# Gate and up projections of a feed-forward layer in pairs by Strassen's algorithm, weight sums by adding transfers and VectorE

## The chip, the cores and the metric

One core of a Trainium2 chip runs the whole program. The metric is the device time of one launch in microseconds (us). TensorE (PE) multiplies, VectorE (DVE) and ScalarE (ACT) work on the results, GpSimd (POOL) does a few products, and SyncE (SP) issues the loads.

## What is computed

A decoder trunk of two layers on 512 tokens of 1024 features, all in float32. Each layer mixes the tokens in four head groups, adds the result to the residual, and then runs the feed-forward part that the change touches:

```python
y = rmsnorm(x, norm2)                          # (512, 1024)
x = x + (silu(y @ w_gate) * (y @ w_up)) @ w_down   # w_gate, w_up: (1024, 2816)
```

## The kernel before

Activations are held feature-major: the residual is eight tiles xT[k] of 128 features x 512 tokens. A weight matrix comes in units of 128 x 1024 floats, 512 KB each: for gate or up, one unit holds 128 output columns, as 8 chunks (k) of 128 x 128. To keep float32 accuracy each operand is split into a high part, rounded to the fast format fp32r, and a low part, the rest; a product is the sum of three matmuls for each k (high·high, low·high, high·low), so a unit has 24 matmuls of 128 x 128 weights against 512 tokens (function `prod`, lines 321, 323 and 325).

Weights are run by the class `Weights`. `load` (L288) issues on SP into one of two raw tiles "wr"; `split` makes the high part by ACT (`S.copy`, L299) and the low part by DVE (L300) into one of three pairs of tiles "wh", "wl"; `get` first prepares until three units stand ready. A load waits until the DVE split has read its raw tile.

The feed-forward part runs over three groups of hidden units, `HID_PARTS` = 0 to 7, 8 to 14, 15 to 21. For each unit j it multiplies gate (g) and up (u), scales the gate's sum by the norm's factors r (DVE, L1145), takes Silu (ACT, L1146), multiplies by r on POOL (L1147), multiplies up's sum by that (DVE, L1150), and splits the product in high and low (ACT L1152, DVE L1153). Then eight units of w_down (d) multiply the group's units, and DVE adds the sums to xT (L1164). The first gate and up unit of a layer wait for nothing but the unscaled operand (`first_two`), and r comes later.

Instructions are written in program order, and a scheduler that has its own idea of durations sets each engine's order when the program is built. That order is fixed in the program: an engine runs its list from the top, and an instruction whose input isn't there holds up all that stand behind it.

## Time and profile before

| | |
|---|---|
| median of 3 runs | 1247.04 us (1246.91 to 1247.53) |
| the profiled execution | 1247.17 us |
| its span, first to last instruction | 1245.5 us |
| granted TensorE clock, mean | 0.998 |
| PE busy | 1231.8 us, 99% |
| DVE, ACT, POOL busy | 698.4, 539.4, 164.6 us |
| weight units loaded | 110 MB moved in all, 88 GB/s |

The first lines of the page give each engine's busy time; the chain of work that ended last says through which engines the end can be followed back. A matmul's row lasts longer than the distance to the next one, since matmuls overlap: what one costs is the distance between two starts in the timeline.

### The profile page before, as it was taken

The numbers are of one execution on the slowest core, as the hardware profiler recorded it, in microseconds if no ns is written. First come the engines' busy times: TensorE is split into PE (matmuls) and PEld (weight loads), VectorE is DVE, ScalarE is ACT, GpSimd is POOL, SyncE is SP. The second block draws the span as 40 slices with busy tenths as digits, with TensorE's granted clock in tenths as the row PEclk, the third lists the DMA queues.
The fourth block names the chain that finished last, engine by engine and source line by source line (L and its number), as shares of the span: only waits on it lengthen the run. The fifth ranks groups of instructions, "written<-read, shape, count | busy, mean of one in ns | idle before, by whom it ended". The sixth has DMA issues, their size and how long they took to land.

```text
span 1245.5 us, 16270 instructions
## 1 busy us (share of the span) xinstructions
PE 1231.8 (99%) x6412; PEld 1009.6 (81%) x6412; DVE 698.4 (56%) x1162; ACT 539.4 (43%) x896; POOL 164.6 (13%) x151
## 2 busy tenths in 40 slices
PE   9999999999999999999999999999999999999997
PEld 7887787788888888888888978777888888888886
DVE  7877798584333334334557678966643343434344
ACT  6557866563222222223444587574532122213232
POOL 0103210001100110111301132000111011101111
PEclk9999999999999999999999999999999999999999
DMA  6222221123323333332333221122233333233321
GB/s 206 93 85 69 60 69 52 52 85 101 102 89 98 102 93 93 102 102 89 98 89 98 86 69 43 53 67 68 86 101 102 91 96 102 89 100 99 97 89 68
DMA packets 32908, 110.00 MB, mean 88 GB/s; under 512 B 4096, under 2 KB 4256, under 8 KB 32832
## 3 DMA queue, kind: packets, MB, share of 16 engines
q1 hardware_dynamic: 31824, 108.28, 28.1%
q8 instruction: 50, 0.82, 0.3%
q10 hardware_dynamic: 432, 0.60, 0.2%
q14 instruction: 26, 0.21, 0.1%
q0 software_dynamic: 576, 0.08, 0.0%
HBM read 106.79 MB, written 2.10 MB: 87 GB/s over the span
## 4 chain that ended last, share of the span: by engine, by line
PE 84%; DVE 7%; ACT 4%; issue 2%; POOL 1%; DMA 0%; SPq 0%; DVEq 0%; POOLq 0%
PE g L325 6%; PE g L323 6%; PE u L323 6%; PE u L325 6%; PE g L321 6%; PE u L321 6%; PE d L325 5%; PE d L323 5%; PE d L321 5%; PE ft L323 3%; PE ft L321 3%; PE ft L325 3%; PE sm L729 2%; PE oa L321 1%; PE oa L325 1%
## 5 line engine op out<-in xcount | busy, mean ns | idle before, releaser
L299 ACT CAST wh<-wr 128x1024 fp32r<-128x1024 f32 (+2 forms) x206 | 210.2, 1022 | 540.4 <-issue 342.5
L300 DVE TENSOR_TENSOR wl<-wr,wh 128x1024 fp32r<-128x1024 f32 (+2 forms) x206 | 244.7, 1188 | 58.2 <-ACT wh L299 57.9
L321 PE MATMUL d<-uh,wh 128*128 128x512 f32 x296 | 115.1, 389 | 0.0
L323 PE MATMUL d<-uh,wl 128*128 128x512 f32 x296 | 115.1, 389 | 0.0
L325 PE MATMUL d<-ul,wh 128*128 128x512 f32 x296 | 115.1, 389 | 0.0
L1150 DVE TENSOR_TENSOR ft<-u,fs 128x512 f32<-128x512 f32 x44 | 30.4, 692 | 131.6 <-PE u L325 127.4
L1164 DVE TENSOR_TENSOR xT<-xT,d 128x512 f32<-128x512 f32 x40 | 27.5, 687 | 104.6 <-PE d L325 104.6
L1147 POOL TENSOR_TENSOR fs<-fs,n_1r 128x512 f32<-128x512 f32 x22 | 38.3, 1743 | 331.9 <-ACT fs L1146 331.9
L1147 POOL TENSOR_TENSOR fs<-fs,n_0r 128x512 f32<-128x512 f32 x22 | 38.3, 1743 | 331.7 <-ACT fs L1146 331.7
L325 PE MATMUL g<-n_0l,wh 128*128 128x512 f32 x176 | 68.5, 389 | 0.0
L323 PE MATMUL g<-n_0h,wl 128*128 128x512 f32 x176 | 68.5, 389 | 0.0
L321 PE MATMUL g<-n_0h,wh 128*128 128x512 f32 x176 | 68.5, 389 | 0.0
L325 PE MATMUL u<-n_0l,wh 128*128 128x512 f32 x176 | 68.5, 389 | 0.0
L321 PE MATMUL u<-n_0h,wh 128*128 128x512 f32 x176 | 68.5, 389 | 0.0
L323 PE MATMUL u<-n_0h,wl 128*128 128x512 f32 x176 | 68.5, 389 | 0.0
L321 PE MATMUL g<-n_1h,wh 128*128 128x512 f32 x176 | 68.5, 389 | 0.0
L323 PE MATMUL g<-n_1h,wl 128*128 128x512 f32 x176 | 68.5, 389 | 0.0
L325 PE MATMUL g<-n_1l,wh 128*128 128x512 f32 x176 | 68.5, 389 | 0.0
L321 PE MATMUL u<-n_1h,wh 128*128 128x512 f32 x176 | 68.5, 389 | 0.0
L323 PE MATMUL u<-n_1h,wl 128*128 128x512 f32 x176 | 68.5, 389 | 0.0
L325 PE MATMUL u<-n_1l,wh 128*128 128x512 f32 x176 | 68.5, 389 | 0.0
L323 PEld LDWEIGHTS d<-uh,wl 128*128 128x128 f32 x296 | 55.6, 188 | 11.6
(669 smaller groups left out, 2815.6 us busy)
## 6 DMA issues: line engine op xcount, KB each, us to landing
wr<-in_weights_dram SPq DMA_DIRECT2D x168, 512.0 KB, 3.5
wr<-in_weights_dram SPq DMA_DIRECT2D x32, 448.0 KB, 3.2
xT<-in_x_dram SPq DMA_DIRECT2D x8, 256.0 KB, 5.6
out_dram<-foo SPq DMA_DIRECT2D x7, 256.0 KB, 2.4
wr<-in_weights_dram SPq DMA_DIRECT2D x6, 256.0 KB, 4.3
posi<-in_positions_dram ACTq DMA_DIRECT2D x1, 256.0 KB, 3.1
out_dram<-foo ACTq DMA_DIRECT2D x1, 256.0 KB, 2.8
fkb<-jrr POOLq DMA_DIRECT2D x8, 4.0 KB, 2.5
```

The source lines that it names most:

```text
L299: S.copy(h[:, c], raw[:, c])
L300: V.tensor_tensor(lo[:, c], raw[:, c], h.bitcast(F32)[:, c], op=ALU.subtract)
L321: PE.matmul(ps, lhsT=wh[:, k, c0:c0 + P], rhs=ah, start=k == 0, stop=False)
L323: PE.matmul(ps, lhsT=wl[:, k, c0:c0 + P], rhs=ah, start=False, stop=False)
L325: last = PE.matmul(ps, lhsT=wh[:, k, c0:c0 + P], rhs=al, start=False, stop=k == n - 1)
L729: PE.matmul(ps[:, :n], lhsT=q[:d, blk(qb)], rhs=k[:d, :n], start=i == 0, stop=i == len(terms[h]) - 1)
L1147: G.tensor_tensor(s, s, r, op=ALU.mult)
L1150: V.tensor_tensor(t, pu, s, op=ALU.mult)
L1164: V.tensor_tensor(xT[m], xT[m], ps, op=ALU.add)
```

## The change

Of the 22 gate and up units of each layer, units 0 to 3 stay as they are ("plain"). The other 18 go in nine pairs, for gate and for up: a pair's weights, 1024 input features x 256 columns, are cut into four quadrants (two feature halves x two column units), and the normalised activations into four (two feature halves x two token halves of 256). Seven products of a quadrant sum against an activation sum (Strassen's algorithm in Winograd's form), each 4 chunks x 3 matmuls of 256 tokens, give what eight would; `pair_products` accumulates them in two PSUM tiles and adds the partial results by three ACT copies and three DVE additions.

The sums of activations are made once a layer (`Halves`), one of four chunk pairs behind each plain unit, on ACT and DVE, from activations that are already multiplied by r, so POOL's product is gone for the pairs.

The sums of weights are made as they arrive. For each product of a pair (gate, then up) SP loads the tiles x and z (and for gate a third, v, which serves both); then POOL issues two transfers of 128 x 512 floats (256 KB) that add another quadrant from memory onto half of x and half of z; two DVE additions make y from x and z. The four parts X, Y, Z and V (two quadrants each, V one) are split in high and low as before. X, Y and Z go round the three pairs of tiles that plain units use, V has its own. The raw tiles x, z, v and y go round six tiles of the ring that held the normalised operand before (`pair_raw`); by this round, x of an up product lands in the tile that held z of the up product before.

The hidden groups become 0 to 7, 8 to 15, 16 to 21: two, four and three pairs.

```diff
@@ -51,7 +51,11 @@
 FRONT_COLS = (GR, GR + 128, SZ, SZ + 128) + tuple(SXBC + 128 * j for j in range(6))
 RINGS = dict(a=8, b=8, c=8, l=8, rg=2, m=2, gv=2, fv=2, as_=4, at=4, g=6, f=6)
 ACT_SET = "natural_log_exp_and_others"
-HID_PARTS = ((0, 8), (8, 15), (15, 22))
+HID_PARTS = ((0, 8), (8, 16), (16, 22))
+
+PLAIN = 4
+HALF = KC // 2
+PAIR_AHEAD = 3
 
 
 def _rope_inv():
@@ -100,12 +104,22 @@
             for i in range(2):
                 add(wout[r0:r0 + 256, 512 * i:512 * i + 512])
         for j0, j1 in HID_PARTS:
-            for j in range(j0, j1):
+            for j in range(j0, min(j1, PLAIN)):
                 add(I["w_gate"][l][:, j * P:j * P + P])
                 add(I["w_up"][l][:, j * P:j * P + P])
+
+            paired[len(units)] = (j1 - max(j0, PLAIN)) // 2, not j0
+            for j in range(max(j0, PLAIN), j1, 2):
+
+                quad = lambda n, r, c: I[n][l][r * D // 2:(r + 1) * D // 2, (j + c) * P:(j + c + 1) * P]
+                for n in ("w_gate", "w_up"):
+                    add(quad(n, 0, 0), quad(n, 0, 1))
+                    add(quad(n, 0, 1), quad(n, 1, 0))
+                    if n == "w_gate":
+                        add(quad("w_gate", 1, 1), quad("w_up", 1, 1))
             for m in range(KC):
                 add(I["w_down"][l, j0 * P:j1 * P, m * P:m * P + P])
-    return np.stack(units), shapes
+    return np.stack(units), (shapes, paired)
 
 
 def _columns(I):
@@ -163,6 +177,15 @@
 
         def ps_acc(name):
             return pa.tile([P, T], F32, tag="pa", name=name)
+
+        slot = [0]
+
+        def act_tile(name, dt=F32R, i=None):
+
+            if i is None:
+                i = slot[0]
+                slot[0] = (i + 1) % 8
+            return ap.tile([P, 1024], dt, tag=f"ap{i}", name=name)
 
         def tmp(tag, name, cols=T, dt=F32, parts=P):
...
             def prefetch(self, n):
-                while (self.n < len(shapes) or self.loaded) and len(self.ready) < n:
+                while (self.n < len(shapes) or self.loaded or self.plan) and len(self.ready) < n:
+                    if not self.loaded and self.n in paired:
+                        self.plan = self.pairs(*paired.pop(self.n))
+                    if self.plan and not self.loaded:
+                        if next(self.plan, None) is None:
+                            self.plan = None
+                        continue
                     for _ in self.split():
                         pass
 
             def get(self):
-                self.prefetch(AHEAD + 1)
+                self.prefetch((PAIR_AHEAD if self.plan else AHEAD) + 1)
                 return self.ready.pop(0)
+
+
+            def pair_raw(self, name):
+                self.raws += 1
+                if self.raws <= 2:
+                    return wp.tile([P, 1024], F32, tag="wr", bufs=RAWS, name=name)
+                return act_tile(name, F32, (self.raws - 3) % 6)
+
+            def pair_part(self, src, name):
+
+                n, i = src.shape[1], self.parts % 4
+                self.parts += 1
+                h, lo = (act_tile(f"{name}{c}", F32R, 6 + j) if i == 3 else
+                         wp.tile([P, 1024], F32R, tag=f"w{c}", bufs=PARTS, name=f"{name}{c}")
+                         for j, c in enumerate("hl"))
+                S.copy(h[:, :n], src)
+                V.tensor_tensor(lo[:, :n], src, h.bitcast(F32)[:, :n], op=ALU.subtract)
+                self.ready.append(tuple(t[:, :n].rearrange("p (k c) -> p k c", c=P) for t in (h, lo)))
+
+            def pair_load(self, both):
+
+                i, wt = self.n, I["weights"]
+                tail = wt[i + 2][:, 0:512] if both else wt[i - 1][:, 512:1024]
+                x, z = self.pair_raw(f"px{i}"), self.pair_raw(f"pz{i}")
+                nc.sync.dma_start(x, wt[i])
+                nc.sync.dma_start(z, wt[i + 1])
+                nc.gpsimd.dma_start(x[:, 512:1024], tail, accum_op=ALU.add)
+                nc.gpsimd.dma_start(z[:, 0:512], wt[i][:, 0:512], accum_op=ALU.add)
+                v = None
+                if both:
+                    v = self.pair_raw(f"pv{i}")
+                    nc.sync.dma_start(v, wt[i + 2])
+                self.n += 3 if both else 2
+                return i, x, z, v
+
+            def pairs(self, n, first):
+
+                if first:
+                    self.raws = 0
+                loads, v = [self.pair_load(True)], None
+                for p in range(2 * n):
+                    i, x, z, vn = loads.pop(0)
+                    v = v if vn is None else vn
+                    self.pair_part(x, f"pX{i}")
+                    yield True
+                    y = self.pair_raw(f"py{i}")
+                    V.tensor_tensor(y[:, 0:512], x[:, 512:1024], x[:, 0:512], op=ALU.add)
+                    V.tensor_tensor(y[:, 512:1024], y[:, 0:512], z[:, 512:1024], op=ALU.add)
+                    self.pair_part(y, f"pY{i}")
+                    yield True
+                    self.pair_part(z, f"pZ{i}")
+                    if p + 1 < 2 * n:
+                        loads.append(self.pair_load(p % 2 == 1))
+                    yield True
+                    self.pair_part(v[:, blk(p % 2, 512)], f"pV{i}")
+                    yield True
...
+        def prod_half(ps, w, act, first=True):
+
+            wh, wl = w
+            for k, (ah, al) in enumerate(act):
+                PE.matmul(ps, lhsT=wh[:, k, :], rhs=ah, start=first and not k, stop=False, skip_group_check=True)
+                PE.matmul(ps, lhsT=wl[:, k, :], rhs=ah, start=False, stop=False, skip_group_check=True)
+                PE.matmul(ps, lhsT=wh[:, k, :], rhs=al, start=False, stop=k == HALF - 1, skip_group_check=True)
+
+        class Halves:
+
+
+
+            def __init__(self, l, g0, r):
+                self.l, self.g0, self.r = l, g0, r
+                names = ("11", "22", "21", "d1", "d2", "d3", "d4")
+                self.act = {n: [] for n in names}
+                self.homes = [t for t in ("c", "l") for _ in range(8)] + ["at"] * 4 + ["as_"] * 4 + ["gv"] * 2 + ["fv"] * 2
+                self.count = 0
+
+            def part(self, name):
+                self.count += 1
+                return [tmp(self.homes.pop(), f"b{name}{c}{self.l}_{self.count}", dt=F32R) for c in "hl"]
+
+            def split(self, src, dst):
+                h, lo = dst
+                S.copy(h, src)
+                V.tensor_tensor(lo, src, h.bitcast(F32), op=ALU.subtract)
+
+            def chunk(self, k):
+                xn = []
+                for i, tag in ((k, "a"), (k + HALF, "b")):
+                    t = tmp(tag, f"xn{self.l}_{i}")
+                    V.scalar_tensor_tensor(t, xT[i], col(self.g0 + i), self.r, op0=ALU.mult, op1=ALU.mult)
+                    xn.append(t)
+                lo, hi = slice(0, 256), slice(256, 512)
+                (b11, b12), (b21, b22) = ((t[:, lo], t[:, hi]) for t in xn)
+                n, d = tmp("g", f"bn{self.l}_{k}"), tmp("g", f"bd{self.l}_{k}")
+                V.tensor_tensor(n[:, lo], b11, b12, op=ALU.subtract)
+                V.scalar_tensor_tensor(n[:, hi], n[:, lo], -1.0, b22, op0=ALU.mult, op1=ALU.subtract)
+                V.tensor_tensor(d[:, lo], b22, b12, op=ALU.subtract)
+                V.scalar_tensor_tensor(d[:, hi], n[:, hi], -1.0, b21, op0=ALU.mult, op1=ALU.subtract)
+                if k % 2 == 0:
+                    self.b11 = self.part("s")
+                at = slice(256 * (k % 2), 256 * (k % 2) + 256)
+                self.split(b11, [t[:, at] for t in self.b11])
+                self.act["11"].append([t[:, at] for t in self.b11])
+                for src, (m, o) in ((n, ("d1", "d2")), (xn[1], ("21", "22")), (d, ("d3", "d4"))):
+                    dst = self.part(m)
+                    self.split(src, dst)
+                    self.act[m].append([t[:, lo] for t in dst])
+                    self.act[o].append([t[:, hi] for t in dst])
+
+        def pair_products(nm, b):
+
+
+            lo, hi = slice(0, 256), slice(256, 512)
+            pa_, pb_ = ps_mix(f"{nm}a"), ps_mix(f"{nm}b")
+            t1, t2 = tmp("f", f"{nm}1"), tmp("f", f"{nm}2")
+            halves = lambda w: [[t[:, 4 * i:4 * i + 4, :] for t in w] for i in range(2)]
+            a11, s1 = halves(W.get())
+            prod_half(pa_[:, lo], a11, b["11"])
+            S.copy(t1[:, lo], pa_[:, lo])
+            prod_half(pb_[:, lo], s1, b["d1"])
+            S.copy(t2[:, hi], pb_[:, lo])
+            s2, s4 = halves(W.get())
+            prod_half(pa_[:, lo], s2, b["d2"], False)
+            S.copy(t1[:, hi], pa_[:, lo])
+            prod_half(pb_[:, lo], s4, b["22"], False)
+            V.tensor_tensor(t1[:, hi], t1[:, hi], pb_[:, lo], op=ALU.add)
+            s3, a12 = halves(W.get())
+            prod_half(pa_[:, lo], s3, b["d3"], False)
+            V.tensor_tensor(t2[:, hi], t2[:, hi], pa_[:, lo], op=ALU.add)
+            prod_half(pb_[:, hi], a12, b["21"])
+            V.tensor_tensor(t1[:, lo], t1[:, lo], pb_[:, hi], op=ALU.add)
+            prod_half(pa_[:, lo], W.get(), b["d4"], False)
+            return t1, t2, pa_[:, lo]
@@ -1135,7 +1297,7 @@
             r = None
             for j0, j1 in HID_PARTS:
                 us = []
-                for j in range(j0, j1):
+                for j in range(j0, min(j1, PLAIN)):
                     pg, pu = ps_proj(f"g{l}_{j}"), ps_mix(f"u{l}_{j}")
                     if r is None:
                         r = norm2.first_two(pg, pu, KC - 2, with_col=False)
@@ -1152,6 +1314,24 @@
                     S.copy(uh, t)
                     V.tensor_tensor(ul, t, uh.bitcast(F32), op=ALU.subtract)
                     us.append((uh, ul))
+                    if j == 0:
+                        quads = Halves(l, 16 + l * 8, r)
+                    quads.chunk(j)
+                lo, hi = slice(0, 256), slice(256, 512)
+                for j in range(max(j0, PLAIN), j1, 2):
+                    s1, s2, end = pair_products(f"g{l}_{j}", quads.act)
+                    S.activation(s1, s1, AF.Silu)
+                    S.activation(s2[:, hi], s2[:, hi], AF.Silu, scale=-1.0)
+                    silu = S.activation(s2[:, lo], end, AF.Silu, scale=-1.0)
+                    t1, t2, end = pair_products(f"u{l}_{j}", quads.act)
+                    V.tensor_tensor(t1, t1, s1, op=ALU.mult)
+                    V.scalar_tensor_tensor(t2[:, hi], t2[:, hi], -1.0, s2[:, hi], op0=ALU.mult, op1=ALU.mult)
+                    V.scalar_tensor_tensor(t2[:, lo], end, -1.0, s2[:, lo], op0=ALU.mult, op1=ALU.mult)
+                    for i, t in enumerate((t1, t2)):
+                        uh, ul = tmp("a", f"uh{l}_{j + i}", dt=F32R), tmp("b", f"ul{l}_{j + i}", dt=F32R)
+                        S.copy(uh, t)
+                        V.tensor_tensor(ul, t, uh.bitcast(F32), op=ALU.subtract)
+                        us.append((uh, ul))
                 if j1 == HC:
                     with tc.issue_after(silu.ins):
```

Where the order of the engines changes, two places matter. In the rows, the numbers behind a name are layer, unit and a buffer's number; px, pz, pv, py are the raw tiles, pXh and pXl the split parts.

**DVE, at the last plain unit, before the first pair.** Before (unit 3 of layer 0, and on to unit 4):

```order
L1153 TENSOR_TENSOR ul0_2_3059<-ft0_2_3022,uh0_2_3058 128x512
L1145 TENSOR_TENSOR ft0_3_3094<-g0_3_3062,n2_0r_2899 128x512
L300 TENSOR_TENSOR wl43_3102<-wr43_3099,wh43_3101 128x1024
L1150 TENSOR_TENSOR ft0_3_3094<-u0_3_3063,fs0_3_3095 128x512
L300 TENSOR_TENSOR wl44_3139<-wr44_3136,wh44_3138 128x1024
L1153 TENSOR_TENSOR ul0_3_3131<-ft0_3_3094,uh0_3_3130 128x512
L1145 TENSOR_TENSOR ft0_4_3166<-g0_4_3134,n2_0r_2899 128x512
L300 TENSOR_TENSOR wl45_3174<-wr45_3171,wh45_3173 128x1024
```

and in the changed kernel, from the same unit on (line numbers are those of the changed kernel):

```order
L387 TENSOR_TENSOR py42_3157<-px42_3116 128x512
L1312 TENSOR_TENSOR ft0_3_3152<-u0_3_3115,fs0_3_3153 128x512
L388 TENSOR_TENSOR py42_3157<-py42_3157,pz42_3117 128x512
L445 SCALAR_TENSOR_TENSOR xn0_3_3203<-xT3_86,pcv_91,n2_0r_2875 128x512
L1315 TENSOR_TENSOR ul0_3_3200<-ft0_3_3152,uh0_3_3199 128x512
L357 TENSOR_TENSOR pY42l_3161<-py42_3157,pY42h_3160 128x1024
L357 TENSOR_TENSOR pZ42l_3165<-pz42_3117,pZ42h_3164 128x1024
L445 SCALAR_TENSOR_TENSOR xn0_7_3205<-xT7_90,pcv_91,n2_0r_2875 128x512
L450 TENSOR_TENSOR bn0_3_3207<-xn0_3_3203 128x256
L452 TENSOR_TENSOR bd0_3_3208<-xn0_7_3205,xn0_3_3203 128x256
L451 SCALAR_TENSOR_TENSOR bn0_3_3207<-bn0_3_3207,xn0_7_3205 128x256
L439 TENSOR_TENSOR bsl0_8_3099<-xn0_3_3203,bsh0_8_3098 128x256
```

The fourth chunk of the activation sums (xn0_3, xn0_7 and what follows) stands behind ft0_3, which waits for the last plain matmul; the first pair product needs bsl0_8, the last row here.

**DVE, in an up product of a pair.** Before (unit 10 of layer 0):

```order
L1153 TENSOR_TENSOR ul0_9_3819<-ft0_9_3782,uh0_9_3818 128x512
L1145 TENSOR_TENSOR ft0_10_3854<-g0_10_3822,n2_0r_2899 128x512
L300 TENSOR_TENSOR wl65_3862<-wr65_3859,wh65_3861 128x1024
L1150 TENSOR_TENSOR ft0_10_3854<-u0_10_3823,fs0_10_3855 128x512
L300 TENSOR_TENSOR wl66_3899<-wr66_3896,wh66_3898 128x1024
L1153 TENSOR_TENSOR ul0_10_3891<-ft0_10_3854,uh0_10_3890 128x512
L1145 TENSOR_TENSOR ft0_11_3926<-g0_11_3894,n2_0r_2899 128x512
```

and in the changed kernel, from the end of the gate product of units 12 and 13 into their up product (73 is that up product's own weights; px75 and px78 are the raw tiles of the next pair's gate and up, and px78 lies where pz73 lay):

```order
L357 TENSOR_TENSOR pZ73l_4597<-pz73_4471,pZ73h_4596 128x1024
L357 TENSOR_TENSOR pV73l_4628<-pv70_4352,pV73h_4627 128x512
L357 TENSOR_TENSOR pX75l_4658<-px75_4600,pX75h_4657 128x1024
L481 TENSOR_TENSOR u0_121_4625<-u0_121_4625,u0_12b_4624 128x256
L388 TENSOR_TENSOR py75_4687<-py75_4687,pz75_4601 128x512
L387 TENSOR_TENSOR py78_4817<-px78_4724 128x512
L484 TENSOR_TENSOR u0_122_4626<-u0_122_4626,u0_12a_4623 128x256
L357 TENSOR_TENSOR pY75l_4691<-py75_4687,pY75h_4690 128x1024
L486 TENSOR_TENSOR u0_121_4625<-u0_121_4625,u0_12b_4624 128x256
L1328 SCALAR_TENSOR_TENSOR u0_122_4626<-u0_122_4626,g0_122_4502 128x256
```

The first addition of py78, which needs px78 with its added half, stands ahead of the addition at L484, which the up product's own PSUM tile waits for.

## Rows read from the trace of the kernel before

**Rows 1.** The page: busy time, share of the span, instructions; and the chain by engine.
```profile
PE 1231.8 (99%) x6412; PEld 1009.6 (81%) x6412; DVE 698.4 (56%) x1162; ACT 539.4 (43%) x896; POOL 164.6 (13%) x151
...
PE 84%; DVE 7%; ACT 4%; issue 2%; POOL 1%; DMA 0%; SPq 0%; DVEq 0%; POOLq 0%
```

**Rows 2.** Busy time by engine over one gate and up unit (us).
```profile
core 0: us, PE busy (x) PEld busy (x) DVE busy (x) ACT busy (x) POOL busy (x), PEclk, DMA share, GB/s
425.70:436.60 10.90, 10.90 (x50) 9.03 (x49) 4.46 (x6) 3.16 (x4) 1.80 (x1) 1.00 0.32 98
```

**Rows 3.** Waits of SP's queue: us in total, times, longest us.
```profile
SPq L288 <- DVE wl L300: 998.2, 186, 14.4
```

**Rows 4.** Timeline of PE, unit u and the next g: start us, us, engine, line.
```profile
429.70 0.39 PE L321 MATMUL u<-n_0h,wh 128*128 128x512 f32 x1
...
434.24 0.39 PE L325 MATMUL u<-n_0l,wh 128*128 128x512 f32 x1
434.46 0.39 PE L321 MATMUL g<-n_0h,wh 128*128 128x512 f32 x1
```

**Rows 5.** Timeline of PE, matmuls against 256 columns.
```profile
85.30 0.28 PE L334 MATMUL fvp<-wh,n_0l 128*128 128x256 f32 x1
85.42 0.28 PE L332 MATMUL fvp<-wh,n_0h 128*128 128x256 f32 x1
...
88.90 0.28 PE L334 MATMUL fvp<-wh,n_0l 128*128 128x256 f32 x1
```

**Rows 6.** Timeline of DVE, two in a row: the second starts 1.15 after the first.
```profile
446.67 1.22 DVE L300 TENSOR_TENSOR wl<-wr,wh 128x1024 fp32r<-128x1024 f32 x1 [0.37 <-ACT wh L299]
447.82 0.69 DVE L1153 TENSOR_TENSOR ul<-ft,uh 128x512 fp32r<-128x512 f32 x1
```

**Rows 7.** Groups by shape: count, busy us, mean ns; then idle before.
```profile
L386 DVE SCALAR_TENSOR_TENSOR n_0l<-xT,pcv,n_0h 128x512 fp32r<-128x512 f32 x16 | 11.7, 748 | 0.8 <-ACT n_0h L385 0.6
L811 DVE TENSOR_TENSOR xT<-xT,dl 128x256 f32<-128x256 f32 x4 | 1.7, 421 | 3.8 <-PE dl L325 3.8
...
L299 ACT CAST wh<-wr 128x1024 fp32r<-128x1024 f32 x168 | 176.2, 1051 | 425.5 <-issue 259.2 <-PE d L325 83.7 <-PE g L325 27.7
L1152 ACT CAST uh<-ft 128x512 fp32r<-128x512 f32 x44 | 27.2, 617 | 4.0 <-DVE ft L1150 4.0
L1015 ACT ACTIVATE fv<-fvp,n_0c 128x256 f32<-128x256 f32 x4 | 1.9, 475 | 4.0 <-PE fvp L334 3.9
```

**Rows 8.** Timeline of PE, the first gate matmul of layer 0.
```profile
259.53 0.39 PE L321 MATMUL g<-n_0h,wh 128*128 128x512 f32 x1
```

**Rows 9.** Timeline of DVE at the first units of layer 0; in brackets the wait.
```profile
277.99 1.23 DVE L300 TENSOR_TENSOR wl<-wr,wh 128x1024 fp32r<-128x1024 f32 x1 [0.23 <-ACT wh L299]
281.30 0.69 DVE L1150 TENSOR_TENSOR ft<-u,fs 128x512 f32<-128x512 f32 x1 [2.08 <-POOL fs L1147]
```

**Rows 10.** Timeline: a last matmul, and the DVE instruction that waited for it.
```profile
1226.48 0.28 PE L325 MATMUL dl<-ul,wh 128*128 128x256 f32 x1
...
1226.80 0.42 DVE L811 TENSOR_TENSOR xT<-xT,dl 128x256 f32<-128x256 f32 x1 [1.61 <-PE dl L325]
```

**Rows 11.** DMA issues: line's tensors, queue, count, KB each, median us to landing.
```profile
wr<-in_weights_dram SPq DMA_DIRECT2D x168, 512.0 KB, 3.5
wr<-in_weights_dram SPq DMA_DIRECT2D x32, 448.0 KB, 3.2
xT<-in_x_dram SPq DMA_DIRECT2D x8, 256.0 KB, 5.6
out_dram<-foo SPq DMA_DIRECT2D x7, 256.0 KB, 2.4
```

**Rows 12.** Timeline of POOL: a DMA issue behind what it waited for.
```profile
47.77 0.54 POOL L1039 DMA_DIRECT2D fkb<-jrr  x1 [0.29 <-POOL fkb L1038]
```

**Rows 13.** DMA issues from POOL between 123 and 128 us.
```profile
w<-in_gla_gate_w_dram POOLq DMA_DIRECT2D x1, 8.0 KB, 2.3
```

More of the change, by code (lines that the diff above doesn't have):

```diff
@@ L67, in _weights @@
 def _weights(I, depth=2):
-    units, shapes = [], []
+    units, shapes, paired = [], [], {}
     def add(*ws):
@@ L133, in _pieces, with trunk @@
     return out
-def trunk(tc, I, out, shapes, depth=2):
+def trunk(tc, I, out, shapes, paired, depth=2):
     nc = tc.nc
@@ L147, in trunk @@
         xp = pool("resid")
-        ap = pool("act", bufs=8)
+        ap = pool("act")
         wp = pool("weights", bufs=3)
@@ L279, in __init__ @@
             def __init__(self):
-                self.loaded, self.ready, self.n = [], [], 0
+                self.loaded, self.ready, self.n, self.plan, self.raws, self.parts = [], [], 0, None, 0, 0
             def load(self, parts=1):
@@ L382, in chunk @@
                 src = xT[k] if src is None else src
-                ah = ap.tile([P, T], F32R, tag="ah", name=f"{name}h{k}")
-                al = ap.tile([P, T], F32R, tag="al", name=f"{name}l{k}")
+                both = act_tile(f"{name}h{k}")
+                ah, al = both[:, 0:T], both[:, T:2 * T]
                 high = S.activation(ah, src, AF.Copy, scale=g)
@@ L446, in mix_operand @@
         def mix_operand(src, name):
-            h = ap.tile([P, T], F32R, tag="ah", name=f"{name}mh")
-            lo = ap.tile([P, T], F32R, tag="al", name=f"{name}ml")
+            both = act_tile(f"{name}mh")
+            h, lo = both[:, 0:T], both[:, T:2 * T]
             S.copy(h, src)
@@ L827, in last_part @@
             for m in range(KC):
-                xg.append(ap.tile([P, T], F32, tag="ah", name=f"xg{m}"))
+                xg.append(act_tile(f"xg{m}", F32)[:, 0:T])
                 ps, w = ps_proj(f"dl_{m}"), W.get()
@@ L1189 @@
     with tile.TileContext(nc) as tc:
-        trunk(tc, I, out, shapes)
+        trunk(tc, I, out, *shapes)
     r = run_bass_kernel_spmd(nc, [arrays], core_ids=[0])
```

## The prediction

> **What bounds the kernel now.** I read the page's busy times and chain first: TensorE is busy for 99% of the span, and 84% of the chain that ended last lies on it [rows 1]. So the time is a count of matmuls times their distance, and a change helps if it makes fewer columns and PE still never waits. The windows then show what room the others have: over one gate and up unit DVE is busy 4.46 us of 10.90 and ACT 3.16 [rows 2]. The waits of SP show that loads stand ready early: its queue waits 998 us for DVE to free a raw tile [rows 3]. What the transfers take is hidden today.
>
> **Fewer columns on PE.** From the first to the last of these rows are 21 starts in 434.46 − 429.70 = 4.76 us, 0.2267 us for a matmul against 512 tokens [rows 4]. Against 256, the 30 starts between 85.30 and 88.90 give 0.120 [rows 5]: a little over half. Two plain units are 48 matmuls, 48 × 0.2267 = 10.88 us. A pair product is 7 products × 4 chunks × 3 = 84 matmuls, 84 × 0.120 = 10.08 us. There are 9 pairs × gate and up × 2 layers = 36, so the gain is 36 × 0.80 = **28.8 us**. The down matmuls only move between groups (8, 8, 6): nothing on a full PE. The Trainium skill (TensorE: Matmul & The Clock Gate, Back-to-back issue gap) gives a lone gap of N/2.4 + 2.5 ns, which I work out as an estimate of 215.8 and 109.2 ns; by it the gain would be 42.8 us. The rows don't bear that out, and I go by 28.8.
>
> **What DVE and ACT get.** Rows that follow one another start 0.07 us before the one ahead has ended: 1024 wide every 1.15 us [rows 6], so 512 wide 0.62 (0.69 less 0.07), with a column factor 0.68 and 256 wide 0.36 [rows 6, 7]. A pair's two products give DVE six 1024-wide splits (6.9), two 512-wide (1.2), four additions for y (2.5), six on PSUM (2.2), and three multiplications and two splits for the result (2.6): 15.4 us of 20.16. ACT has six 1.05, two 0.62, six copies of some 0.45, Silu and two casts: 13. Both fit; what counts is where they stand in order. POOL's product falls away, which was on no path.
>
> **A wait before the first pair.** The first unit's matmuls begin at 259.53 [rows 8], so the plain units end at 259.53 + 4 × 10.88 = 303.05. DVE writes the first up product at 281.30 [rows 9]. From there its list up to the first part of y holds 18 instructions of 0.62, 6 of 0.68, 15 of 0.36 and 3 of 1.15: 24.1 us, to 305.4, 2.4 after PE has ended the plain units. Only then come ft0_3 and ten more rows, 7.0 us together, to bsl0_8, the last chunk of the first product's operand: 312.4. PE has 18 matmuls that need only the first three chunks (2.2 us), then waits. The other 66 take 7.9, and the copies between them, which a late product no longer hides (ACT's cast of the next weights stands among them), some 1.5 more: 321.8 instead of 313.1, less 0.6 for five matmuls that the order takes from the next product. That is 8.1 a layer, **+16.2 us**. The least is 5.7 a layer, if DVE isn't behind at 303.05 (8.1 less 2.4), the most 9.6, if the copies cost twice as much.
>
> **A loop through the raw tiles.** Time 0 is the first matmul of an up product; a group of 12 takes 1.44, so the fifth ends at 7.20 and the seventh, which accumulates onto what L484 reads, should begin at 8.64. DVE's list has the first y addition for the next up product just ahead of L484. That addition needs the next x, and x lands in the tile of this product's z. In the gate product before, at its 7.20 + 0.2 for the signal (1226.48 + 0.12 to 1226.80 [rows 10]), DVE still has a 1024-wide split to end; L484 is over at about 8.6, ACT's Silu at 9.0, its cast of z at 10.05, DVE's split of z at 11.3: 1.2 in the up product's time. SP's load takes 3.5 [rows 11], with 0.05 for the signal to 4.75. POOL wakes 0.29 later [rows 12] and issues the adding transfer, which takes A. At 5.04 + A the addition (0.62) and L484 (0.42) can go. They had to begin by 7.55, so **PE waits A − 2.5** in that product. Behind L484 DVE holds the split of Y, due 4 us later, and behind POOL's transfer the one for z, due later still; these have cover. The loop closes over z's split again, so it costs this in every pair but the last of a group: 5 a layer (units 8, 10, 12, 16, 18), 10 in all. In the first of units 4 to 7 the addition stands behind L484: nothing is counted there.
>
> A is not in this trace. Nearest below is a store of 256 KB, 2.4 us [rows 11]; nearest in kind a load by POOL of 8 KB, 2.3 us [rows 13]. 448 and 512 KB by SP differ by 0.3 [rows 11], so 256 KB are worth 1.2 and a plain load by POOL 2.3 + 1.2 = 3.5. An addition must read its target too: if that costs the transfer again, 4.7. Loads of 256 KB in the opening crowd took 5.6 [rows 11], the upper end. I take **A = 3.7**, near the row's 3.5, since only the second read is missing there. Then PE waits 1.2 in 10 products: **+12 us**. The Trainium skill (DMA: Bandwidth & Descriptors, Anatomy of one DMA) fits 2.0 us + bytes/436e3 for transfers from GpSimd; as an estimate 2.6 us here, with which this term would be 1 us; no run here shows an adding transfer.
>
> In a group's first pair the gate's y addition stands ahead of z's split too: its x waits for Z's split 2.5 after the down part, so it comes at 2.5 + 0.05 + 3.5 + 0.29 + 3.7 = 10.0 in the gate product, and the z split ends at 10.0 + 0.62 + 0.4 + 1.15 = 12.2, or 2.1 instead of 1.2: 0.9 × 2 groups × 2 layers = **+3.6**.
>
> **Sum.** −28.8 + 16.2 + 12 + 3.6 = +3.0. The profiled execution took 1247.17 us (span 1245.5), 0.13 above the median of the runs. The forecast is **1250.2 us**.
>
> **Rivals.**
> - *The transfers keep up.* A of 2.4 to 2.8: the loop costs 0 to 3, and −28.8 + 16.2 leaves −12.6: **1235** to 1238. For it: a store of this size takes 2.4. Against: POOL's own transfers need 2.3 for 8 KB.
> - *The first pair isn't held.* If ACT and DVE reach the fourth chunk in time, and the start costs at most 4 in all where I count 16.2, 1250.2 − 12.2 = **1238**. Against: the list is fixed, and DVE is full from 281.
> - *The adding transfers are slow* (the other side in full). The seventh group of each up product waits for POOL's transfer. The loop passes the gain where 10 (A − 2.5) + 4 × (A − 2.8) reaches 12.6, at A = 3.5. At A = 4.5 it costs 20 + 6.8: **1261**; at 5.6, 31 + 11.2: **1277**. For it: two loads of 512 KB and another addition are under way at the same time, where today one is.
> - *DVE falls behind.* With 15.4 of 20.2 us in strict order, every signal adds; 0.3 us more in each of 18 pairs on top of my forecast gives **1256**, and a granted clock at the lower of its two levels (1.2 instead of 2.4 GHz) after the wait in front of the first pair would add to it. The rows show the clock at 1.00 [rows 2], never after a wait of 7 us.
>
> **How the numbers follow.** My forecast, A from 3.0 to 4.5, has 0.42: 1240 to 1261, of which I give 0.02 to faster, 0.12 to no change, 0.28 to slower. Transfers that keep up: 0.26, faster. The start not held: 0.09, of which 0.08 faster and 0.01 unchanged. Slow transfers: 0.16, slower. DVE behind: 0.07, of which 0.01 unchanged. A measurement here tells 0.2%, 2.5 us, from no change. So faster 0.36, same 0.14, slower 0.50. The range is **1234 to 1264**: from A = 2.4 to 4.7. It leaves out most of the slow transfers, and what lies below 1234 if both the first two rivals hold, under 2 in 10 together.
>
> **What would show it.** In the changed profile: pair matmuls 0.120 apart; a stretch of some 7 us in each layer, after the fourth plain unit, in which PE does nothing and waits for DVE's low parts of the activation sums (their names begin with bs and bd); POOL's 256 KB transfers with a time to landing of 3 to 4.5; and PE's waits in the up products of units 8, 10, 12, 16 and 18, right before the seventh group, with DVE's y addition ended just before. I am wrong if PE waits elsewhere (on ACT's copies, or on weights at the start of a product), or if these transfers land within 2.5 us.

## The result, and the profile after

The changed kernel takes **1321.69 us** (median of 4 runs, 1318.49 to 1322.87) beside 1247.28 for the kernel before on the same chip: a ratio of 1.0592, 95% interval 1.0573 to 1.0612. It is 74 us slower, where 3 were forecast. The profiled execution took 1322.36 us, its span is 1320.6.

The page of the changed kernel: busy time, share of the span, instructions; PE's granted clock in 40 slices; the chain by engine and by line.

```profile
PE 1240.7 (94%) x7702; PEld 1077.1 (82%) x7702; DVE 863.0 (65%) x1476; ACT 650.0 (49%) x1126; POOL 166.4 (13%) x187
...
PEclk9999999998999899989999999999989989899999
...
PE 53%; issue 15%; DMA 12%; DVE 11%; ACT 6%; POOL 2%; SPq 0%; DVEq 0%; POOLq 0%; ACTq 0%
```

Against [rows 1] PE fell from 99% of the span to 94%, and from 84% of the chain to 53%. DMA, 0% of the chain before, has 12. And the clock has slices below 9: PE's 1240.7 us busy hold fewer columns than the 1231.8 of before, partly at the lower clock.

Busy time by stretch in the changed kernel (PE, PEld, DVE, ACT, POOL, then granted clock, DMA share, GB/s): the start of the first pair, and most of the four pairs of the middle group.

```profile
304.00:320.00 16.00, 8.09 (x42) 7.25 (x41) 13.74 (x24) 8.07 (x15) 4.88 (x4) 0.71 0.89 249
410.00:500.00 90.00, 80.69 (x614) 79.33 (x614) 54.88 (x79) 41.96 (x71) 12.15 (x14) 0.92 0.57 141
```

Two places lose time: a stop of some 8 us at the first pair, with DVE busy for 13.74 of 16 us, and a steady loss over all pairs, in which no engine is full (PE 80.69 and DVE 54.88 of 90). PE's waits name them. Columns: us in total, times, longest.

```profile
PE g_4a L417 <- ACT bsh L438: 11.7, 2, 6.2
PE u_8a L417 <- DVE u L484: 7.5, 2, 3.8
...
PE u_12a L417 <- DVE u L484: 6.0, 2, 3.8
PE g_4a L419 <- DVE bsl L439: 4.7, 2, 2.4
```

The first and the last are the fourth chunk of the activation sums. The others stand before the seventh product of an up product, behind L484, where the prediction had put them; but they are 1.7 to 3.8 us instead of 1.2, and there are 15 of them instead of 10. From PE's timeline I added up how long each of the 36 pair products takes beyond its 84 × 0.120 = 10.08 us: **100.8 us** in all. Of these, 64.9 are waits (16.4 of them for the activation sums of the first pairs), 26.9 are matmuls at 0.21 instead of 0.12, the rest small steps. Less the 28.8 of gain that makes 72.0 of the 74.4 found.

What L484 stands behind is seen on DVE in one up product (start, us, what, in brackets the wait):

```profile
478.73 0.69 DVE L388 TENSOR_TENSOR py<-py,pz 128x512 f32<-128x512 f32 x1 [2.17 <-DMA pz<-in_weights_dram]
479.99 0.69 DVE L387 TENSOR_TENSOR py<-px 128x512 f32<-128x512 f32 x1 [0.56 <-DMA px<-in_weights_dram]
480.60 0.41 DVE L484 TENSOR_TENSOR u<-u,u_12a 128x256 f32<-128x256 f32 x1
```

The first is the second y addition of the next gate product, waiting for z; the second is the addition that the prediction looked at, waiting for x. Over the ten up products that the prediction counted, DVE waits 23.0 us before L388 and 12.4 before L387: z holds L484 up longer than x does.

Why both come late is read from the chain over one pair, in order of time (start, us, what; smaller pieces, of up to 0.52 us, are left out at the marks):

```profile
446.78 0.70 DVE pV68l L357
...
447.50 4.96 DMA pz<-in_weights_dram
...
452.50 0.49 issue
452.99 4.73 DMA pz<-in_weights_dram
...
457.87 1.05 ACT pZ70h L356
...
458.94 1.24 DVE pZ70l L357
...
460.20 4.23 DMA px<-in_weights_dram
...
464.50 0.49 issue
464.98 3.56 DMA px<-in_weights_dram
...
469.02 0.10 DVE py L387
...
469.63 0.42 DVE g L486
...
470.08 0.63 ACT g L1323
...
470.98 0.52 ACT pV73h L356
...
471.52 0.70 DVE pV73l L357
```

PE isn't in it. The split of V frees the tile into which z is loaded (4.96); POOL issues the adding transfer into z (0.49 + 4.73); Z is cast and split; that frees the tile for the next x, which is loaded (4.23) and added to (0.49 + 3.56); then come the first y addition, the gate's own addition behind it, Silu, and the cast and split of the next V. This last leg is one of order alone: V's cast needs nothing of x, but in the lists L486 stands behind L387 on DVE, and V's cast behind Silu on ACT. From one split of V to the next are 471.52 − 446.78 = **24.7 us per pair**, of which 17.5 are the four transfers. PE needs 20.2. The kernel runs at the pace of this round.

The transfers themselves (KB, median us to landing):

```profile
px<-in_weights_dram SPq DMA_DIRECT2D x36, 512.0 KB, 3.6
pz<-in_weights_dram SPq DMA_DIRECT2D x36, 512.0 KB, 4.9
px<-in_weights_dram POOLq DMA_DIRECT2D x36, 256.0 KB, 4.5
...
pz<-in_weights_dram POOLq DMA_DIRECT2D x36, 256.0 KB, 5.9
```

An adding transfer takes 4.5 to 5.9 where 3.7 was assumed, and the plain load of z beside it 4.9 where loads took 3.5 [rows 11].

### The profile page after: what moved, and what is told of

Its sections match the earlier page's. It is cut to its first block, busy times and chain, and to the rows that moved or that the text cites. A ratio compares the mean times of both kernels' runs of the same rounds, so it can differ in the third digit from the quotient of the medians.

```text
span 1320.6 us, 19692 instructions
## 1 busy us (share of the span) xinstructions
PE 1240.7 (94%) x7702; PEld 1077.1 (82%) x7702; DVE 863.0 (65%) x1476; ACT 650.0 (49%) x1126; POOL 166.4 (13%) x187
## 4 chain that ended last, share of the span: by engine, by line
PE 53%; issue 15%; DMA 12%; DVE 11%; ACT 6%; POOL 2%; SPq 0%; DVEq 0%; POOLq 0%; ACTq 0%
DMA px<-in_weights_dram 7%; PE d L406 5%; PE d L408 5%; PE d L410 5%; DMA pz<-in_weights_dram 5%; PE ft L408 3%; PE ft L406 3%; PE ft L410 3%; DVE wl L323 1%; DVE xn L445 1%; PE dl L406 1%; PE dl L410 1%; PE dl L408 1%; PE fvp L496 1%; PE fvp L494 1%
## 5 line engine op out<-in xcount | busy, mean ns | idle before, releaser
L322 ACT CAST wh<-wr 128x1024 fp32r<-128x1024 f32 (+2 forms) x134 | 134.4, 1004 | 214.4 <-PE d L410 94.3
L323 DVE TENSOR_TENSOR wl<-wr,wh 128x1024 fp32r<-128x1024 f32 (+2 forms) x134 | 156.4, 1167 | 35.0 <-ACT wh L322 34.8
L367 POOL DMA_DIRECT2D px<-in_weights_dram x36 | 31.3, 870 | 383.3 <-DVE g L481 226.3
L406 PEld LDWEIGHTS d<-uh,wh 128*128 128x128 f32 x304 | 57.9, 191 | 11.9
L410 PEld LDWEIGHTS d<-ul,wh 128*128 128x128 f32 x304 | 57.5, 189 | 12.2
L368 POOL DMA_DIRECT2D pz<-in_weights_dram x36 | 31.6, 877 | 168.6 <-DMA pz<-in_weights_dram 74.0
L388 DVE TENSOR_TENSOR py<-py,pz 128x512 f32<-128x512 f32 x36 | 24.8, 690 | 38.0 <-DMA pz<-in_weights_dram 37.8
L387 DVE TENSOR_TENSOR py<-px 128x512 f32<-128x512 f32 x36 | 24.9, 691 | 32.6 <-issue 17.4
L406 PE MATMUL ft<-n_0h,wh 128*128 128x512 f32 x80 | 31.9, 398 | 0.6 <-ACT wh L322 0.6
L408 PE MATMUL ft<-n_0h,wl 128*128 128x512 f32 x80 | 31.7, 396 | 0.0
L410 PE MATMUL ft<-n_0h,wh 128*128 128x512 f32 x80 | 31.4, 392 | 0.0
L408 PE MATMUL ft<-n_1h,wl 128*128 128x512 f32 x80 | 31.3, 392 | 0.0
L406 PE MATMUL ft<-n_1h,wh 128*128 128x512 f32 x80 | 31.3, 391 | 0.0
L410 PE MATMUL ft<-n_1h,wh 128*128 128x512 f32 x80 | 31.2, 390 | 0.0
L1137 DVE SCALAR_TENSOR_TENSOR fa<-cv,pcv,fa 128x511 f32<-128x511 f32 (+2 forms) x36 | 26.9, 748 | 0.7
L1139 ACT ACTIVATE fo<-fa 128x512 f32<-128x512 f32 x20 | 12.4, 630 | 30.3 <-DVE fa L1137 30.2
```

The costliest lines, as they stand in the source:

```text
L322: S.copy(h[:, c], raw[:, c])
L323: V.tensor_tensor(lo[:, c], raw[:, c], h.bitcast(F32)[:, c], op=ALU.subtract)
L367: nc.gpsimd.dma_start(x[:, 512:1024], tail, accum_op=ALU.add)
L368: nc.gpsimd.dma_start(z[:, 0:512], wt[i][:, 0:512], accum_op=ALU.add)
L387: V.tensor_tensor(y[:, 0:512], x[:, 512:1024], x[:, 0:512], op=ALU.add)
L388: V.tensor_tensor(y[:, 512:1024], y[:, 0:512], z[:, 512:1024], op=ALU.add)
```

## The experiments

Twelve kernels, timed in three rounds each against the kernel before. "Beyond 10.08" is the sum over the pair products as above (for the 12 added matmuls, beyond 10.08 and their own 1.44). The scheduler orders each of these kernels anew, so an edit can move VectorE's list too; where that bears on a reading, it is said. The ratios are to the kernel before, with their 95% intervals.

| kernel | us | ratio | beyond 10.08 | waits of PE in them |
|---|---|---|---|---|
| the change | 1321.7 | 1.0573 to 1.0612 | 100.8 | 64.9 |
| no adding transfers | 1245.1 | 0.9978 to 0.9996 | 26.9 | 16.0 |
| none into x | 1276.4 | 1.0221 to 1.0258 | 55.8 | 36.0 |
| none into z | 1292.6 | 1.0347 to 1.0390 | 71.6 | 49.0 |
| eight raw tiles | 1268.4 | 1.0156 to 1.0187 | 46.5 | 30.4 |
| 12 matmuls in the wait | 1321.9 | 1.0584 to 1.0616 | 73.8 | 54.3 |
| two parts ahead | 1316.3 | 1.0531 to 1.0566 | 97.7 | 63.3 |
| six plain units | 1301.2 | 1.0411 to 1.0454 | 78.1 | 47.0 |
| sums on GpSimd | 1312.0 | 1.0505 to 1.0538 | 83.6 | 67.2 |
| sums on VectorE | 1254.7 | 1.0044 to 1.0075 | 28.3 | 19.3 |
| eight tiles, six units | 1249.3 | 1.0009 to 1.0038 | 30.1 | 17.6 |
| the same, sums on GpSimd | 1251.7 | 1.0023 to 1.0045 | 27.8 | 16.5 |
| the same, sums on VectorE | **1230.7** | 0.9853 to 0.9883 | 6.9 | 3.3 |

**Without the adding transfers.**

```diff
-                nc.gpsimd.dma_start(x[:, 512:1024], tail, accum_op=ALU.add)
-                nc.gpsimd.dma_start(z[:, 0:512], wt[i][:, 0:512], accum_op=ALU.add)
```

> Both adding transfers of each pair product are left out, so the weight sums hold only their first addend; all else stays. Theory L (the waits before the seventh product of the up products, 44 us in all, come from the round through the raw tiles, whose longest part is the adding transfer): these waits and the lower clock behind them go, the stop before the first pair stays (23.7 us above the ideal in two layers): 1247.3 - 28.8 + 24 + some 5 for the rest = 1247 us, 1240 to 1256. Theory D (VectorE's and ScalarE's lists in their fixed order set the pace, whoever adds): little changes, over 1300 us.

Measured 1245.1, as theory L had it. Its middle pairs, busy time as above, and PE's two longest waits:

```profile
412.00:432.00 20.00, 20.00 (x168) 19.94 (x167) 15.70 (x23) 11.29 (x19) 0.00 (x0) 1.00 0.40 125
```

```profile
PE g_4a L415 <- ACT bsh L436: 10.0, 2, 5.0
PE g_4a L417 <- DVE bsl L437: 4.7, 2, 2.4
```

PE never stands still there, with the same work on DVE and ACT; only the first pair stops. ACT's list is the same, DVE's has the y additions at other places, in the up products both of them still ahead of L484. So the adding transfers, with what the scheduler made of them, cost 1321.7 − 1245.1 = 76.6 us, and theory D falls; the run without z's transfer, below, bears that out with DVE's list as it was. The row also gives the rest of the balance: 1247.0 − 28.8 + 26.9 is 1245.1 again. Of the 26.9, the gate and up products of the first pair have 21.3 (10.4 in one layer and 10.9 in the other).

**One of the two left out.** With the line for x, then the line for z removed:

> Only the adding transfer into x (second half) is left out, so those sums hold their first addend alone. Theory L1 (as the prediction had it: only x's transfer stands in the round that PE waits for): all that both together cost goes, 1245 to 1252 us. Theory L2 (x's and z's transfers stand one behind the other in one round of a pair, through V's tile and Z's tile): the round of some 25 us loses 5 and stands at about the 20.2 that PE needs: 1250 to 1275 us.

> Only the adding transfer into z (first half) is left out, so those sums hold their first addend alone. Theory L1: z's transfer has cover, little changes: 1305 to 1322 us. Theory L2: it is half of what lengthens the round: 1250 to 1280 us.

Measured 1276.4 and 1292.6: 45.3 and 29.1 less than the change, 74.4 together, about what both bring at once. Neither had cover, so L1 falls. But L2 has the sizes wrong as well: 1276.4 is 1.4 above its range, and 1292.6 lies 12.6 above it, between the ranges of both theories. The round with one adding transfer still isn't below PE's own 20.2 us: behind the first pair, the pairs take 20.3 to 23.8 us without x's and 20.4 to 25.1 without z's. In the chain of the kernel without x's, one round from V's split to V's split takes 457.00 − 434.60 = 22.4 us, 9.1 of them z's two transfers and the rest mainly work of ACT and DVE in the order of their lists.

The price of z's transfer is the clean one. Without it the lists of PE, ACT and DVE are those of the change, but for one y addition a layer; and the kernels without x's and without both differ by two exchanges a layer on DVE and one on ACT. The first two differ by 29.1 us, the other two by 1276.4 − 1245.1 = 31.3: some 30 us for a transfer that the prediction had given cover. Without x's transfer DVE's list changes (the next gate's y addition no longer stands ahead of L486), so its 45.3 us are transfer and order together.

**Two tiles more.** The two tiles of the plain units' loads lie idle during the pairs; here they join the ring.

```diff
-                if self.raws <= 2:
+                i = (self.raws - 1) % 8
+                if i < 2:
                     return wp.tile([P, 1024], F32, tag="wr", bufs=RAWS, name=name)
-                return act_tile(name, F32, (self.raws - 3) % 6)
+                return act_tile(name, F32, i - 2)
```

> The two raw tiles that the plain units use join the six of the pairs: eight raw tiles where a pair takes seven. The transfers stay as they are. Theory L: each load can go two tiles earlier, the transfers' 5 us lie beside the work of a product before, and only the stop before the first pair stays: 1245 to 1260 us. Rival B (the adding transfers cost through the traffic itself, whenever they go): 1300 us or more.

Measured 1268.4, 53 us less than the change. The adding transfers in it:

```profile
px<-in_weights_dram POOLq DMA_DIRECT2D x36, 256.0 KB, 4.8
...
pz<-in_weights_dram POOLq DMA_DIRECT2D x36, 256.0 KB, 4.7
```

They still take long (x's 4.8 where it took 4.5, z's 4.7 where it took 5.9), but hold PE up far less: it takes 10.2 us for most products. That refutes rival B and speaks for the loop. The ring isn't all that changed: the scheduler also put the y additions to other places in DVE's list, behind the gate's L486 and earlier in the up product, and this run doesn't part the two. It missed the upper end of L by 8 us for a second stop that I hadn't foreseen:

```profile
PE g_10a L418 <- ACT g L475: 10.1, 2, 5.3
```

It comes once a layer. In the kernel with eight tiles and six units it lies where three loads and three adding transfers overlap one another between 428 and 443 us and one of the latter takes 7.3 us (issued at 434.76; DVE's addition behind it starts at 442.15). It is gone in the last kernel below, which has no adding transfers.

**Matmuls in the wait.** In each up product the sixth product is computed once more, into a half of PSUM that nobody reads after.

```diff
             prod_half(pb_[:, hi], a12, b["21"])
+            if nm[0] == "u":
+                prod_half(pb_[:, lo], a12, b["21"])
```

> In every up product PE computes the sixth product once more, into a part of PSUM that nobody reads afterwards, right before the seventh: 12 matmuls, 1.44 us, inside the wait. Theory C (the clock falls because PE had stood still, and the lower clock, 27 us in all, is on the path): waits of 2 to 4 us shrink to 1 to 2.5, fewer matmuls at the lower clock behind them: 1300 to 1315 us. Theory L alone (the transfers' round sets the pace, and what the clock costs is absorbed by the next wait): 1318 to 1326 us. If the waits didn't cover the added matmuls: up to 18 x 2 x 1.44 / 2 = 26 us more.

First what the clock does in the changed kernel: behind the wait of 3.76 us matmuls stand 0.21 apart, and 0.12 again from 437.08 on.

```profile
431.38 0.58 PE L417 MATMUL u_8a<-bd3h,pV63h 128*128 128x256 f32 x1 [3.76 <-DVE u L484]
...
434.11 0.41 PE L417 MATMUL g_10a<-bsh,pX65h 128*128 128x256 f32 x1
434.32 0.41 PE L418 MATMUL g_10a<-bsh,pX65l 128*128 128x256 f32 x1
...
437.08 0.28 PE L419 MATMUL g_10b<-bd1l,pX65h 128*128 128x256 f32 x1
437.20 0.28 PE L417 MATMUL g_10b<-bd1h,pX65h 128*128 128x256 f32 x1
```

```profile
433.00:437.00 4.00, 4.00 (x21) 4.00 (x20) 2.41 (x5) 1.66 (x3) 0.00 (x0) 0.50 0.53 143
```

The granted clock is 0.50 there: the lower level, 1.2 GHz. With the matmuls in the wait the same window of the middle group runs at 1.00:

```profile
410.00:500.00 90.00, 81.01 (x658) 79.20 (x657) 55.29 (x79) 42.10 (x70) 12.97 (x15) 1.00 0.61 152
```

The matmuls at 0.21 lose only 10.9 us over all pairs instead of 26.9, and the time is the same, 1321.9. Waits and clock loss fell by 10.6 + 16.0 = 26.6, and the 216 added matmuls take 25.9. So in the pairs the lower clock follows from the waits and is hardly an addend of its own: a product that PE ends sooner only waits longer. That is theory L alone. One reserve: in the up products of units 4 and 20 there was no wait left for the added matmuls, 4 × 1.44 = 5.8 us, and a gain from the clock of up to that size could hide behind them.

**Two parts ahead.** `PAIR_AHEAD = 3` becomes 2.

> The weights of the pairs are prepared two parts ahead instead of three; transfers, additions and tiles stay. The y additions stand later against the seventh product's addition (L484) on VectorE, so that L484 isn't behind them. Theory Q (PE waits only because L484 stands behind an addition that waits for a transfer): the waits before the seventh products shrink, 1280 to 1305 us. Theory L2 (the transfers' round itself is longer than PE's work): the wait only moves to another place: 1312 us or more.

1316.3, in L2's range: waits of 63.3 instead of 64.9 us, most still before the seventh product, and 7.6 at a new place, in the product g_6. But the edit didn't do what it was made for. In the up products of units 8, 10, 12, 16 and 18 both y additions still stand ahead of L484 in DVE's list; in unit 12 they start at 478.09 (L388) and 479.34 (L387), L484 at 479.94. So theory Q is not tested by any run here. What speaks against it is the chain over one pair above, which closes from V's split to V's split without L484 of an up product.

**Six plain units.**

```diff
-PLAIN = 4
+PLAIN = 6
...
-                    quads.chunk(j)
+                    if j < HALF:
+                        quads.chunk(j)
```

> Six plain units ahead of the first pair instead of four (16 units in pairs), the activation sums still spread over the first four. Theory S (the stop before the first pair is VectorE's fourth chunk alone): the first pair's 23.7 us above the ideal fall away, 4 pair products fewer cost 3.2, and the waits of one pair per layer (some 8 and 6) go as well: 1290 to 1302 us. Rival: the stop only moves, because the first sums of weights come late by themselves: 1310 us or more.

1301.2, within theory S: PE no longer waits for the activation sums in any row. In the first pair another stop is left:

```profile
PE g_6a L417 <- ACT g L479: 8.8, 2, 4.6
```

The copy L479 stands on ACT behind the cast of the next product's x:

```profile
334.24 1.05 ACT L356 CAST pX49h<-px 128x1024 fp32r<-128x1024 f32 x1 [5.74 <-DMA px<-in_weights_dram]
335.19 0.36 ACT L479 COPY g<-g_6a 128x256 f32<-128x256 f32 x1
```

So the stop behind DVE's fourth chunk goes, and another one, of the transfers, shows at the first pair.

**The sums on chip.** Both addends are loaded anyway, so that the sums need no second transfer.

```diff
+                    E.tensor_tensor(x[:, 512:1024], x[:, 512:1024], v[:, blk(p % 2, 512)], op=ALU.add)
                     self.pair_part(x, f"pX{i}")
...
+                    E.tensor_tensor(z[:, 0:512], z[:, 0:512], x[:, 0:512], op=ALU.add)
                     self.pair_part(z, f"pZ{i}")
```

with E GpSimd, then VectorE:

> The adding transfers are replaced by two additions of 128x512 on GpSimd from tiles that are loaded anyway. Theory L: an addition of 1.6 to 2.0 us on GpSimd stands where 0.87 + 4.5 to 5.9 us of transfer stood; the round of two products gets some 7 us shorter, below the 20.2 us that PE needs: like without the transfers or up to 10 us more, 1247 to 1260 us. Theory D: over 1300 us, since nothing is taken from VectorE.

> As with the additions on GpSimd, but on VectorE, 0.62 us each in the place of 1.5 to 1.8: VectorE has 17.9 of 20.2 us to do per pair. Theory L2: the round loses 0.87 + 4.5 and 0.87 + 5.9 and gets 1.2 for them: 1250 to 1275 us. Theory D2 (an on-chip addition costs as much by its place in the fixed order, since z's sum then holds x's tile longer and every y waits for it): 1295 to 1320 us, as on GpSimd (1312).

1312.0 and 1254.7. On VectorE the time is in theory L2's range, 67 us less than the change. On GpSimd theory L missed by over 50: there the additions cost nearly what the transfers did, and the time is in theory D's range, though the run without the transfers had refuted D. One addition took 1.5 (x) and 1.7 us (z) at the median, on VectorE 0.69:

```profile
L390 POOL TENSOR_TENSOR pz<-pz,px x36: 1254/1707/2267, 300.1 to 1240.1; 128x512 f32<-128x512 f32 x36
L382 POOL TENSOR_TENSOR px<-px,pv x36: 1254/1492/4378, 306.5 to 1236.4; 128x512 f32<-128x512 f32 x36
```

```profile
L382 DVE TENSOR_TENSOR px<-px,pv 128x512 f32<-128x512 f32 x8 | 5.5, 686 | 2.9 <-DMA px<-in_weights_dram 2.9
```

Four a pair make 2 × (1.5 + 1.7 − 1.4) = 3.6 us; the two kernels differ by (83.6 − 28.3) / 18 = 3.1 a pair. That fits an addition that lies in the round. But the lists differ too: with GpSimd the next up product's y addition stands ahead of L484, on VectorE behind it, so how much of the 57 us is the length of the addition isn't shown. Why the round with GpSimd is longer than PE's work, its chain shows:

```profile
435.29 1.14 DVE pZ65l L357
...
446.62 1.24 DVE pZ68l L357
...
454.79 1.73 POOL pz L390
...
459.63 1.15 DVE pZ70l L357
```

It is another round, through z's tile in both products: the split of Z frees the tile of the next x, which is loaded (4.77, then 3.57) and added to on GpSimd, and behind y's additions comes the next split of Z. From gate to gate that is 459.63 − 435.29 = 24.3 us, 5.0 of them additions on GpSimd, beside PE's 20.2.

**Together.**

> Eight raw tiles and six plain units together. If both causes are apart and add: the gain of 32 products, 25.6 us, less some 3 to 8 for what stays at the first pairs: 1224 to 1232 us, below the kernel before. If the stop at the first pair of six plain units (some 7 us a layer, in the product with Z) has its own cause: 1236 to 1242 us.

> The same with the sums of weights on GpSimd, 1.5 to 1.8 us each, 6.6 us per pair on an engine that has nothing else there: 1224 to 1232 us if the adding transfers were the cause of the two stops; 1240 us or more if a slow addition in the chain of x and y holds PE up even with the deeper ring.

> Eight raw tiles, six plain units, the sums of weights on VectorE and no adding transfer. If what stayed with eight tiles and six units (one stop of 3 to 5 us in the middle group of a layer and one in the first pair) comes from the adding transfers: 1247.1 - 25.6 + 2 to 8 = 1224 to 1230 us. If VectorE's order holds PE up: 1240 us or more.

The first came out above both of its cases, at 1249.3: the stop at the first pair stays (8.6 us in two layers) and so does the one in the middle group (8.2). Both are gone in the last, which at **1230.7 us** beats the kernel before by 1.3% and misses its range by 0.7. Its middle group and what follows:

```profile
391.00:510.00 119.00, 119.00 (x838) 111.97 (x837) 85.14 (x121) 53.94 (x83) 0.00 (x0) 1.00 0.37 118
```

PE is full at clock 1.00. With GpSimd in its place 1251.7, in the case in which a slow addition holds PE up even with the deeper ring.

## Why the prediction was wrong

- **The gain, 28.8: right.** Pair matmuls are 0.120 apart, and with 1247.0 − 28.8 and what PE's timeline shows beyond 10.08 the kernel without adding transfers comes out to 0.1 us. Where nothing waits a product takes 10.08 to 10.25: without the adding transfers all products behind the first pairs have 5.6 us beyond 10.08 together, which the sum didn't have.
- **The wait before the first pair, 16.2: right in kind, too small.** PE waits for bsh and bsl as foretold. Without adding transfers the first pairs take 21.3 us too long over two layers, 14.7 of them waits. In the change DVE ends the first layer's bsl at 315.1 (314.69 + 0.42) where its list gave 312.4: the list held no waits, and DVE had two, of 1.19 and 1.16 us, for POOL's product and one of 0.46 for ACT. With the clock at 0.71 in the 16 us from 304 on, the rest of the product took longer too.
- **The loop through the raw tiles, 12 + 3.6: this step failed.** The adding transfers cost 76.6. The place was right, the seventh product of the up products behind L484 and the y addition, and the sentence that failed is the one on z: "behind POOL's transfer the one for z, due later still; these have cover". z's transfer, counted at nothing, cost 29.1 us with the lists as they were. I followed the loop from the split of z at a fixed 1.2 us of the up product, as if PE's pace set that split. It is itself the end of V's split, z's load and z's adding transfer. The measured round of 24.74 us has 7.26 that aren't transfers; with the durations that I had assumed, 2 × (3.5 + 3.7), it comes to 21.7, which is 1.5 more than PE's 20.2 in each of 18 pairs, an estimate of 27 us where 15.6 were forecast. So the missing leg alone would have given some 1262, still inside the range; with A too small as well the time went far outside.
- **A, assumed 3.7: too small where it counted.** With one load beside it (issued at 345.89, between 340 and 352 us) the adding transfer into x landed in 3.7; over all 36 the medians are 4.5 and 5.9. The bound of 5.6 from the opening crowd [rows 11] was the nearer row. The rival "the adding transfers are slow" named the traffic as the reason and gave up to 1277; it had the same single leg. The two durations together, 17.5 instead of 14.4 us of transfer, bring the round from 21.7 to 24.7, or 4.6 a pair beyond PE's 20.2: over 18 pairs an estimate of 82, beside the 76.6 measured. The pairs aren't alike: those of units 6 to 19 take 23.1 to 27.8 us, the last of a layer some 21.5.
- **"Nothing is counted" for units 4 to 7 and the last pair of a group: wrong.** u_6 waited 2.9 and 3.3, u_14 2.5 and 1.9. In a group's last pair the first y of the next group stands ahead of L484 (its second addition started at 504.22, after waiting 2.60 for z). Units 4 and 5 had no such wait in one layer and 1.7 in the other; only units 20 and 21 had none in either.
- **The clock, assumed 1.00: wrong**, 0.92 over the middle group; but as the matmuls in the wait show, that cost little by itself in the pairs, at most some 6 us.

The Trainium skill (DMA: Bandwidth & Descriptors, Issuing engines are not separate DMA queues) says that transfers started from GpSimd and from SP run on the same 16 DMA engines and interleave. The rows bear that out for z, whose plain load, in flight together with the adding transfers, took 4.9 us and without them 4.0. x's load took 3.6 and 4.0, so it shows no such loss; 16 of its 36 ran with no adding transfer in flight, of z's 5. The fit on the same page of the Trainium skill (Anatomy of one DMA), which gave an estimate of 2.6 us, does not hold for an adding transfer here: none of the 72 landed in less than 3.6. Without the adding transfers:

```profile
px<-in_weights_dram SPq DMA_DIRECT2D x36, 512.0 KB, 4.0
pz<-in_weights_dram SPq DMA_DIRECT2D x36, 512.0 KB, 4.0
```

## What to carry to other kernels

Where a ring of buffers closes over transfers, add up the whole round, from one release of a tile back to its next release, and compare it with what the busiest engine needs; a leg that "has cover" at the old pace may be what sets the new one. A transfer that adds is priced by a row taken under the traffic it will run in; if both addends are on chip already, an addition on VectorE in front of its user was cheaper here (1254.7 instead of 1321.7 us, with another order of VectorE's list). A ring with one tile more than a full turn uses took most of the transfers off the path (1268.4), again with another order. An order of instructions can be a leg of a round just as a buffer can, and an edit that is to change the order has to be read back from the trace.

## What the hardware showed

- An adding transfer of 256 KB took 3.7 us beside one load and 4.5 to 5.9 at the median of the pairs. Between 405 and 500 us POOL's queue (nearly all adding) used 21.9% of the DMA engines for 3.41 MB, SP's 34.0% for 9.71: 6.4 and 3.5% per MB.

```profile
q1 hardware_dynamic: 2658, 9.71, 34.0%
q0 software_dynamic: 1872, 3.41, 21.9%
```

- PE's clock stood at the lower level behind the waits of the up products, for 25 matmuls behind the one of 3.76 us; 12 matmuls in the waits kept it up in the first layer's middle group, and the time stayed at 1321.9.
- An addition of 128x512 on GpSimd took 1.25 to 2.3 us for nearly all, one 4.4, on VectorE 0.69.
